# SBUF pools placed from both ends of the partition in a two-block float32 transformer kernel

## The chip, the core and the metric

The kernel runs on one NeuronCore of one Trainium2 chip. The metric is the time of one execution on the device in microseconds (us); less is better. Engines are named as in the profile: PE (TensorE matmuls), PEld (its weight loads), DVE (VectorE), ACT (ScalarE), POOL (GpSimd) and SP (the queue that issues most DMAs). SBUF addresses below are kilobytes (KB) from the start of a partition; every partition has the same layout.

## What is computed

One transformer block (differential attention and latent attention side by side, then a SwiGLU feed-forward) on 256 tokens of width 1024, and after it two layers of a second block. Everything is float32. Cut to its matrix products:

```python
z = rms_norm(x) @ w_in                      # q, k, v, latents, gates
y_a = merge_heads(diff_attention(z)) @ w_proj_a
y_b = merge_heads(latent_attention(z)) @ w_proj_b
x = x + rms_norm((sigmoid(g_a) * y_a + sigmoid(g_b) * y_b) @ w_o)
x = x + rms_norm((silu(n(x) @ w_ffn_gate) * (n(x) @ w_ffn_up)) @ w_ffn_down)
for i in range(2):                          # the second block's layers
    h = h + 0.5 * rms_norm(swiglu(n(h), gate[i, 0], up[i, 0], down[i, 0]))
    h = h + rms_norm((retention if i == 0 else stick_breaking)(n(h)))   # each ends in "@ w_out"
    h = h + 0.5 * rms_norm(swiglu(n(h), gate[i, 1], up[i, 1], down[i, 1]))
    h = h + rms_norm(sigmoid(n(h) @ ple_w_gate[i]) * (p[i] @ ple_w_proj[i]))
```

So there are five feed-forwards (hidden width 2816 = 22 x 128), and some 280 MB of weights go through the core once.

## The kernel before

**Three matmuls for one.** A float32 operand is split into two rounded halves of type float32r, `hi` and `lo`; a product is `hi*hi + hi*lo + lo*hi`, so three PE instructions in place of one. Weights come in chunks of 2048 columns (`chunk`): one DMA of 1 MB from SP into a buffer of the pool `raw` (3 buffers `w_raw`), then for each 512 columns a cast on ACT (L188) into `w_hi` (pool `hip`, 12 buffers) and a subtraction on DVE (L189) into `w_lo` (pool `lop`, 12 buffers).

**Two forms of product.** In the form by tokens (`tokens` and `token_steps`, instructions of L197) the stationary operand, the one that PE loads as weights, is 128x128 of the activations and the moving operand is 512 (sometimes 256) columns of `w_hi` or `w_lo`. In the form by features (`mat_steps`, L214) the weights are stationary and 256 tokens of the activations move. The names of the activations: `x_hi`/`x_lo` is the normed input of every stage, `a_*` the hidden layer of a feed-forward (stationary in the down-projection, 22 blocks x 2 token halves x 2 output halves x 3 = 264 instructions in each of five feed-forwards), `u_*` the retention's output, `o_*` the stick-breaking's, `oa_*` and `ob_*` the two attentions', `m_*` their sum, `pe_*` the extra embedding, `cq_*`/`ckv_*` the latents, `p_*` and `v_*` the retention's scores and values (there `v` moves). Full float32 matmuls are left for transposes (`xt`, `at`, `mt`, ...: the identity in `kc` moves, the tile to be turned is stationary) and for attention scores. `h` is the residual stream, read by the transposes of every stage.

**What sets the order.** The order on each engine is fixed when the program is built, by the place in the code and by priorities; tiles of a pool are handed out in that order, and a tile that takes the place of an older one waits until the older one's readers are done. Pools that stay for the whole program lie one behind the other from the low end in the order of their creation (`const`, `raw`, `hip`, `lop`, `act`, `sm`, `tmp`); the pools of a stage (`mix`, `big`, `ends`, `ret`, `stick`, `emb`) are stacked behind them, and dropped at the stage's end. `h` is a tile of `act`.

Of the kernel before, what the change touches and what calls it, by code (L numbers as in the profile page):

```python
# [10 lines left out]
F32 = mybir.dt.float32  # L11
# [7 lines left out]
P = 128  # L19
T = 256  # L20
D = 1024
# [73 lines left out]
class Weights:  # L95


    def __init__(self):
        self.parts = []
# [45 lines left out]
class Build:  # L145
    def __init__(self, ctx, tc, aps):
        self.ctx, self.tc, self.nc = ctx, tc, tc.nc
        self.aps = aps
        self.plan = []
        self.at = 0  # L150
        pool = lambda name, bufs, **k: ctx.enter_context(tc.tile_pool(name=name, bufs=bufs, **k))
        self.const = pool("const", 1)
        self.raw = pool("raw", 3)
        self.hip = pool("hip", WB)
        self.lop = pool("lop", WB)
        self.act = pool("act", 1)
        self.sm = pool("sm", 2)
        self.tmp = pool("tmp", 2)
        self.psm = pool("psm", 4, space=PSUM)
        self.psa = pool("psa", 4, space=PSUM)  # L160
        self.filler, self.behind, self.late = Filler(), None, []
        self.later = None
# [337 lines left out]

    def setup(self):
        nc, const, aps = self.nc, self.const, self.aps
        self.h = self.act.tile([P, 2, D], F32, name="h", tag="h")

        self.h0 = self.h.rearrange("p b d -> p (b d)").rearrange("p (k t) -> p k t", k=KT)
        self.vecs = const.tile([P, NV], F32, name="vecs")
        self.kc = const.tile([P, NK], F32, name="kc")
        nc.scalar.dma_start(self.kc[:, :P], aps["kc"][:, :P])
        nc.scalar.dma_start(self.vecs[:, :KT], aps["vecs"][:, :KT])
        self.pos = self.tmp.tile([P, T], I32, name="pos", tag="s")  # L510
        self.lam = self.tmp.tile([P, 4 * 64], F32, name="lam", tag="s")
        self.ident = self.kc[:, K_ID : K_ID + P]
        self.ones = const.tile([P, P], F32, name="ones")
        nc.vector.memset(self.ones, 1.0)
        self.dummies(WARM[0])
        self.mhalf = const.tile([P, 2], F32, name="mhalf")
        nc.vector.memset(self.mhalf, -0.5)
# [777 lines left out]
    def run(self):  # L1295
        tc = self.tc
        self.setup()
        g2 = lambda i, n: self.vec(V_G2 + (i * 8 + n) * 8, 8)
        row = lambda i, n: R_G2 + 4 * i + n // 2
        stage = self.first()  # L1300
        with tc.tile_pool(name="big0", bufs=1) as self.big:
            self.ffn(*stage, ("w_ffn_gate", "w_ffn_up", "w_ffn_down"), (0,), R_FFN, 1.0)
        names = ("ffn_w_gate_2", "ffn_w_up_2", "ffn_w_down_2")
        out = self.aps["out"].rearrange("p (b d) -> p b d", b=2)
        p_halves = self.ctx.enter_context(tc.tile_pool(name="p_halves", bufs=1))
        self.pe = [p_halves.tile([P, SUB], F32R, name=f"pe_{x}") for x in "hl"]
        pos = self.tmp.tile([P, T], I32, name="pos", tag="s")
        self.nc.gpsimd.dma_start(pos, self.aps["pos2"].to_broadcast([P, T]))
        self.table2 = self.rope_table("2", pos, self.kc[:, K_F2 : K_F2 + 1], self.const)
        for i in range(2):  # L1310
            with tc.tile_pool(name=f"big{i}a", bufs=1) as self.big:
                self.ffn(*self.next_stage(g2(i, 0)), names, (i, 0), row(i, 1), 4.0)
            self.later = lambda i=i: self.embed_in(i)
            mixer = self.stick if i else self.retention
            mixer(*self.next_stage(g2(i, 2)), row(i, 3))
            with tc.tile_pool(name=f"emb{i}", bufs=1) as emb:
                e = emb.tile([P, 2, D], F32, name="e")
                self.embed(i, e)
                with tc.tile_pool(name=f"big{i}b", bufs=1) as self.big:
                    self.ffn(*self.next_stage(g2(i, 4)), names, (i, 1), row(i, 5), 4.0)  # L1320
                self.ple(i, *self.next_stage(g2(i, 6), 4.0), e, row(i, 7), out if i else None)
        assert self.at == WCOLS * P, (self.at, WCOLS * P)
# [66 lines left out]
```

## Time and profile before

| | |
|---|---|
| median of 3 runs | 1613.9 us (1613.33 to 1614.34) |
| the profiled execution's own time | 1613.39 us |
| its span, first to last instruction | 1611.5 us |
| PE busy in the span | 1597.7 us (99%) |
| PE's share of the chain that ended last | 95% |
| DVE, ACT, POOL busy | 1065.2, 904.1, 79.9 us |
| DMA, mean | 179 GB/s |

The span is what the trace covers; about 2 us of the execution lie around it. Busy time of PE is the time in which a matmul was under way, and matmuls overlap (a 512-column one is shown with some 390 ns, though another starts every 230 ns), so a busy PE is not yet a PE at its best pace. Its pace is read from the starts of consecutive instructions in the timeline, or from a piece of the chain of work: a piece that is "x243" long and lasts 56.70 us takes 56.70 / 243 us for each instruction.

### The profile page before, as it was taken

To read this page: it belongs to the slowest core of one execution; us is meant where nothing else is said; L and a number is where in the kernel's file an instruction comes from. 1 tells how busy PE (TensorE), PEld (TensorE's weight loads), DVE (VectorE), ACT (ScalarE), POOL (GpSimd) and SP (SyncE) were. 2 spreads that over 40 slices of the span, in tenths; PEclk is the share of its full clock that TensorE was granted. 3 is DMA by queue.
4 is the path that set the end of the run, shared out by engine and by line. 5 is a ranking of instruction groups with operands and counts; after the bars stand their busy time and mean duration, and the time that the engine had idled before them with its cause. 6 is when DMAs were issued, how large, how long until landed. Compare 5 with 4: busy or idle time off the path is not lost.

```text
span 1611.5 us, 22515 instructions
## 1 busy us (share of the span) xinstructions
PE 1597.7 (99%) x8230; PEld 1344.3 (83%) x8230; DVE 1065.2 (66%) x1969; ACT 904.1 (56%) x1792; POOL 79.9 (5%) x97
## 2 busy tenths in 40 slices
PE   9999999999999999999999999999999999999997
PEld 8898778888888888898888888878888899888886
DVE  7987766765566665777766555486665677666546
ACT  6665544755455554645546555476554656655545
POOL 0000000200001000100000000012000200000001
PEclk9999999999999999999999999999999999999999
DMA  7535436455546555555455555555555554455552
GB/s 243 211 123 190 167 106 221 183 179 201 183 159 220 183 183 183 167 189 183 160 190 179 187 178 188 183 198 200 183 183 183 176 192 149 165 183 183 183 175 73
DMA packets 47134, 288.72 MB, mean 179 GB/s; under 512 B 5968, under 2 KB 9168, under 8 KB 14384
## 3 DMA queue, kind: packets, MB, share of 16 engines
q1 hardware_dynamic: 44528, 279.29, 49.3%
q0 software_dynamic: 2064, 7.80, 1.4%
q8 instruction: 64, 1.05, 0.3%
q14 instruction: 46, 0.38, 0.1%
q10 hardware_dynamic: 432, 0.20, 0.0%
HBM read 284.78 MB, written 1.05 MB: 177 GB/s over the span
## 4 chain that ended last, share of the span: by engine, by line
PE 95%; DVE 2%; DMA 1%; issue 1%; ACT 1%; SPq 0%; POOL 0%; POOLq 0%; DVEq 0%; ACTq 0%
PE ps L197 78%; PE ps L214 9%; PE at L628 1%; PE S L660 1%; PE xt L429 1%; DMA w_raw<-in_w 1%; DVE w_lo L189 1%; PE o L197 1%; PE o L707 0%; DMA h<-in_x 0%; PE S L1073 0%; PE S L1187 0%; PE pt L697 0%; PE o L834 0%; PE ot L1110 0%
## 5 line engine op out<-in xcount | busy, mean ns | idle before, releaser
L189 DVE TENSOR_TENSOR w_lo<-w_raw,w_hi 128x512 fp32r<-128x512 f32 x1054 | 708.8, 687 | 348.8 <-ACT w_hi L188 343.5
L188 ACT CAST w_hi<-w_raw 128x512 fp32r<-128x512 f32 x1054 | 639.6, 621 | 489.2 <-PE ps L197 355.8
L197 PE MATMUL ps<-w_hi,x_hi 128*128 128x512 f32 (+1 forms) x1280 | 488.9, 382 | 0.3 <-ACT x_hi L433 0.3
L197 PE MATMUL ps<-w_hi,x_lo 128*128 128x512 f32 (+1 forms) x1280 | 483.0, 377 | 0.5 <-DVE x_lo L435 0.5
L197 PE MATMUL ps<-w_lo,x_hi 128*128 128x512 f32 (+1 forms) x1280 | 482.1, 377 | 0.0
L197 PEld LDWEIGHTS ps<-w_hi,x_lo 128*128 128x128 f32 x1280 | 240.8, 188 | 46.9 <-DVE x_lo L435 2.1
L197 PEld LDWEIGHTS ps<-w_hi,x_hi 128*128 128x128 f32 x1280 | 241.0, 188 | 43.3 <-issue 1.0
L197 PEld LDWEIGHTS ps<-w_lo,x_hi 128*128 128x128 f32 x1280 | 241.2, 188 | 42.1
L197 PE MATMUL ps<-w_hi,a_hi 128*128 128x512 f32 x440 | 176.7, 402 | 0.0
L197 PE MATMUL ps<-w_hi,a_lo 128*128 128x512 f32 x440 | 173.3, 394 | 0.0
L197 PE MATMUL ps<-w_lo,a_hi 128*128 128x512 f32 x440 | 172.6, 392 | 0.0
L296 POOL TENSOR_TENSOR r<-v,mhalf 128x1 f32<-128x1 f32 (+1 forms) x50 | 61.4, 1228 | 1262.6 <-DVE v L384 1097.7
L214 PE MATMUL ps<-x_hi,w_hi 128*128 128x256 f32 x440 | 114.8, 289 | 0.7 <-ACT x_hi L356 0.5
L214 PE MATMUL ps<-x_hi,w_lo 128*128 128x256 f32 x440 | 112.5, 284 | 0.6 <-DVE w_lo L189 0.6
L197 PEld LDWEIGHTS ps<-w_hi,a_lo 128*128 128x128 f32 x440 | 82.6, 188 | 21.3
L197 PEld LDWEIGHTS ps<-w_lo,a_hi 128*128 128x128 f32 x440 | 82.7, 188 | 19.2
L197 PEld LDWEIGHTS ps<-w_hi,a_hi 128*128 128x128 f32 x440 | 82.6, 188 | 18.4
L214 PEld LDWEIGHTS ps<-x_hi,w_hi 128*128 128x128 f32 x440 | 84.0, 191 | 2.2 <-issue 0.7
L214 PEld LDWEIGHTS ps<-x_hi,w_lo 128*128 128x128 f32 x440 | 84.1, 191 | 1.5 <-DVE w_lo L189 1.2
L623 DVE SCALAR_TENSOR_TENSOR a<-ps,R,s 128x512 f32<-128x512 f32 (+1 forms) x60 | 42.2, 703 | 55.4 <-PE ps L197 44.0
L214 PE MATMUL ps<-x_lo,w_hi 128*128 128x256 f32 x440 | 77.4, 283 | 0.0
L270 ACT CAST a_hi<-at 128x512 fp32r<-128x512 f32 (+1 forms) x60 | 33.1, 551 | 70.4 <-PE at L628 70.4
(271 smaller groups left out, 1484.0 us busy)
## 6 DMA issues: line engine op xcount, KB each, us to landing
w_raw<-in_w SPq DMA_DIRECT2D x254, 1024.0 KB, 4.9
gr<-in_rows POOLq DMA_DIRECT2D x10, 512.0 KB, 4.1
w_raw<-in_w SPq DMA_DIRECT2D x7, 512.0 KB, 3.4
w_raw<-in_w SPq DMA_DIRECT2D x12, 256.0 KB, 5.1
w_raw<-in_w SPq DMA_DIRECT2D x6, 384.0 KB, 3.3
h<-in_x SPq DMA_DIRECT2D x4, 256.0 KB, 5.6
h<-in_x POOLq DMA_DIRECT2D x1, 1024.0 KB, 8.9
out<-h SPq DMA_DIRECT2D x3, 256.0 KB, 2.5
```

The costliest lines, as they stand in the source:

```text
L188: nc.scalar.copy(hi[:, :m], r[:, c0:c1])
L189: nc.vector.tensor_sub(lo[:, :m], r[:, c0:c1], hi[:, :m].bitcast(F32))
L197: mm = lambda a, b, **k: nc.tensor.matmul(ps, a, b, skip_group_check=True, **k)
L214: mm = lambda *a, **k: self.nc.tensor.matmul(*a, skip_group_check=True, **k)
L270: nc.scalar.copy(hi, src)
L296: self.nc.gpsimd.tensor_tensor(r, v, self.mhalf[:, :n], op=ALU.pow)
L429: nc.tensor.transpose(pt[:, i, :], self.h[:, b, k * P : (k + 1) * P], self.ident)
L623: nc.vector.scalar_tensor_tensor(a, banks[1], R[:, b : b + 1], s, op0=ALU.mult, op1=ALU.mult)
L628: nc.tensor.transpose(pt[:, i, :], a[:, i * P : (i + 1) * P], self.ident)
L660: mm(S[:, at], q[:, qs], k[:, ks], start=n == 0, stop=n == len(parts[0]) - 1, skip_group_check=True)
```

## The change

The pools are given a side. `hip`, `lop`, `act` and the pools of the stages stay on the left (the low end); `const`, `raw`, `sm`, `tmp`, `p_halves` (the tiles `pe_*`) and `emb` go to the right and are stacked from the high end down. `h` moves from `act` into a pool of its own, `res`, on the right. No instruction is added, removed or given another shape.

```diff
-        self.const = pool("const", 1)
-        self.raw = pool("raw", 3)
+
+        self.const = pool("const", 1, side="right")
+        self.raw = pool("raw", 3, side="right")
         self.hip = pool("hip", WB)
         self.lop = pool("lop", WB)
         self.act = pool("act", 1)
-        self.sm = pool("sm", 2)
-        self.tmp = pool("tmp", 2)
+        self.res = pool("res", 1, side="right")
+        self.sm = pool("sm", 2, side="right")
+        self.tmp = pool("tmp", 2, side="right")
...
-        self.h = self.act.tile([P, 2, D], F32, name="h", tag="h")
+        self.h = self.res.tile([P, 2, D], F32, name="h", tag="h")
...
-        p_halves = self.ctx.enter_context(tc.tile_pool(name="p_halves", bufs=1))
+        p_halves = self.ctx.enter_context(tc.tile_pool(name="p_halves", bufs=1, side="right"))
...
-            with tc.tile_pool(name=f"emb{i}", bufs=1) as emb:
+            with tc.tile_pool(name=f"emb{i}", bufs=1, side="right") as emb:
```

The addresses that the two built programs give to the tiles, in KB of a partition:

| tile | read by PE as | before | after |
|---|---|---|---|
| `kc` (identity), `ones` | moving, float32 | 16.8 to 17.9 | 220.8 to 221.9 |
| `w_raw` | (not by PE) | 20.0 to 44.0 | 196.1 to 220.1 |
| `w_hi` | moving (L197), stationary (L214) | 44.0 to 68.0 | 16.1 to 40.1 |
| `w_lo` | moving (L197), stationary (L214) | 68.0 to 92.0 | 40.1 to 64.1 |
| `h` | stationary, float32 | 92.0 to 100.0 | 188.1 to 196.1 |
| `x_hi`, `x_lo`; `ob_*` in the same place | stationary (L197), moving (L214) | 100.0 to 116.0 | 64.1 to 80.1 |
| `a_hi`, `a_lo` | stationary | from 133.1, 137.1 or 145.1, to 189.1 at most | 80.1 to 124.1 |
| `u_h`, `u_l` | stationary | 137.1 to 169.1 | 80.1 to 112.1 |
| `oa_h`, `oa_l` | stationary | 145.1 to 161.1 | 92.1 to 108.1 |
| `m_h`, `m_l` | stationary | 161.1 to 177.1 | 108.1 to 124.1 |
| `o_h`, `o_l` | stationary | 148.6 to 164.6 | 91.6 to 107.6 |
| `pe_h`, `pe_l` | stationary | 133.1 to 137.1 | 167.0 to 171.0 |
| `ckv_*` / `cq_*` | both / moving | 196.1 to 200.1 / 190.1 to 196.1 | 143.1 to 147.1 / 137.1 to 143.1 |
| retention's `p_*` / `v_*` | stationary / moving | 205.6 to 211.6 / 169.1 to 185.1 | 148.6 to 154.6 / 112.1 to 128.1 |
| `a` (before its transpose) | stationary, float32 | 181.1 to 197.1 | 128.1 to 132.1 |

On PE, DVE, ACT and SP the instructions stand in the same order in both programs. PE in the first feed-forward of the second block, with what it waits for in brackets (`at` is the transpose of the hidden layer; the numbers of lines are two higher in the changed file). Before:

```order
L197 MATMUL ps<-w_hi,x_hi 128x512
L197 MATMUL ps<-w_lo,x_hi 128x512
L197 MATMUL ps<-w_hi,x_lo 128x512
L628 MATMUL at<-kc,a 128x128 [waits DMASW3_49,DVE_49]
L628 MATMUL at<-kc,a 128x128 x3
L197 MATMUL ps<-w_hi,x_hi 128x512 [waits Activation_49]
```

After:

```order
L199 MATMUL ps<-w_hi,x_hi 128x512
L199 MATMUL ps<-w_lo,x_hi 128x512
L199 MATMUL ps<-w_hi,x_lo 128x512
L630 MATMUL at<-kc,a 128x128 [waits DVE_49]
L630 MATMUL at<-kc,a 128x128 x3
L199 MATMUL ps<-w_hi,x_hi 128x512 [waits Activation_49]
```

One wait for a DMA of POOL's queue (`DMASW`) is gone there; the tile `a` no longer lies where that DMA had written. POOL is the one engine with another order. It loads the gain rows of each stage (`gr`, 512 KB). Before, at the end of the first layer:

```order
L467 DMA gr<-in_rows 128x1024
L296 TENSOR_TENSOR r<-v_10532,mhalf 128x1
L467 DMA gr<-in_rows 128x1024 x2
L296 TENSOR_TENSOR r<-v_10630,mhalf 128x1
L453 COPY R<-r 128x1
```

After, the same place, and behind "..." the place at the end of the stick-breaking stage to which one of the two loads goes:

```order
L469 DMA gr<-in_rows 128x1024
L298 TENSOR_TENSOR r<-v_10535,mhalf 128x1
L469 DMA gr<-in_rows 128x1024
L298 TENSOR_TENSOR r<-v_10633,mhalf 128x1
...
L298 TENSOR_TENSOR r<-v_13824,mhalf 128x1
L469 DMA gr<-in_rows 128x1024
L298 TENSOR_TENSOR r<-v_13990,mhalf 128x1
```

It is the gain row of the last feed-forward, which is first read about 200 us behind the new place.

## Rows read from the trace of the kernel before

**Rows 1.** The page: busy time, granted clock in 40 slices, chain by engine.

```profile
PE 1597.7 (99%) x8230; PEld 1344.3 (83%) x8230; DVE 1065.2 (66%) x1969; ACT 904.1 (56%) x1792; POOL 79.9 (5%) x97
...
PEclk9999999999999999999999999999999999999999
...
PE 95%; DVE 2%; DMA 1%; issue 1%; ACT 1%; SPq 0%; POOL 0%; POOLq 0%; DVEq 0%; ACTq 0%
```

**Rows 2.** Waits of PE, the longest: total us, times, longest us.

```profile
PE dummy L522 <- DVE mhalf L517: 1.1, 1, 1.1
```

**Rows 3.** The chain of work, longest pieces: start us, us, what, how many.

```profile
418.01 56.70 PE ps L197 x243
...
821.08 48.06 PE ps L197 x206
```

**Rows 4.** The chain in 318 to 342 us, products with `x`.

```profile
317.85 16.32 PE ps L197 x72
```

**Rows 5.** The chain in 240 to 290 us: `ob`, then `m`.

```profile
243.61 1.40 PE ps L197 x6
245.66 8.88 PE ps L197 x39
...
268.11 17.50 PE ps L197 x75
```

**Rows 6.** Busy us (x instructions) PE, PEld, DVE, ACT, POOL; clock, DMA share, GB/s.

```profile
420.00:460.00 40.00, 40.00 (x173) 32.20 (x172) 20.14 (x30) 18.15 (x30) 0.00 (x0) 1.00 0.56 196
340.00:380.00 40.00, 40.00 (x184) 33.11 (x183) 22.85 (x34) 21.25 (x36) 0.00 (x0) 1.00 0.56 199
```

**Rows 7.** PE's groups by shape, xcount | busy us, mean ns | idle.

```profile
L197 PE MATMUL ps<-w_hi,x_hi 128*128 128x512 f32 x1120 | 442.9, 395 | 0.3 <-ACT x_hi L433 0.3
...
L197 PE MATMUL ps<-w_hi,a_hi 128*128 128x512 f32 x440 | 176.7, 402 | 0.0
...
L197 PE MATMUL ps<-w_hi,u_l 128*128 128x512 f32 x64 | 25.6, 400 | 0.0
```

**Rows 8.** Chain, short pieces: `oa`, `x`, `a` behind an interruption; then `o`, `pe`.

```profile
218.51 1.40 PE ps L197 x6
...
311.86 2.78 PE ps L197 x12
...
604.10 2.79 PE ps L197 x12
...
1371.96 17.06 PE ps L197 x73
```

**Rows 9.** Chain, other PE work: retention's `p`/`v`; transposes of `a`, of `h`; L214.

```profile
707.23 2.08 PE o L197 x9
...
311.42 0.44 PE at L628 x4
...
285.61 0.87 PE xt L429 x8
...
678.74 11.51 PE ps L214 x96
```

**Rows 10.** Timeline of PE, 166 to 168 us: `cq` moving, six instructions apart.

```profile
166.50 0.28 PE L214 MATMUL ps<-cq_h,w_hi 128*128 128x256 f32 x1
...
167.20 0.28 PE L214 MATMUL ps<-cq_h,w_hi 128*128 128x256 f32 x1
```

**Rows 11.** The page: cast, subtraction; weight DMAs (KB, us to landing).

```profile
L189 DVE TENSOR_TENSOR w_lo<-w_raw,w_hi 128x512 fp32r<-128x512 f32 x1054 | 708.8, 687 | 348.8 <-ACT w_hi L188 343.5
L188 ACT CAST w_hi<-w_raw 128x512 fp32r<-128x512 f32 x1054 | 639.6, 621 | 489.2 <-PE ps L197 355.8
...
w_raw<-in_w SPq DMA_DIRECT2D x254, 1024.0 KB, 4.9
```

**Rows 12.** Timeline of POOL at the end of the first layer.

```profile
1064.28 0.53 POOL L467 DMA_DIRECT2D gr<-in_rows  x1 [1.22 <-DVE h L415]
1064.82 0.82 POOL L296 TENSOR_TENSOR r<-v,mhalf 128x1 f32<-128x1 f32 x1
```

## The prediction

> **What bounds the kernel now.** The page comes first: PE is busy 1597.7 us of 1611.5, and the chain that ended last is PE for 95% [rows 1]. The longest wait of PE is 1.1 us [rows 2], so there is hardly a stall to remove. A change can gain only if PE's instructions themselves follow each other faster, or lose if they follow slower or begin to wait. So the next view is the pace of PE, and the chain gives it without any modelled end: length of a piece over its count. Four readings for the same shape, 128x128 stationary and 512 columns moving, all of line L197:
> - down-projection, `a` stationary: 56.70 / 243 = 233.3 ns [rows 3];
> - retention's output, `u` stationary: 48.06 / 206 = 233.3 ns [rows 3];
> - any product with `x` stationary: 16.32 / 72 = 226.7 ns [rows 4];
> - the two products of the first block's end, a few us apart and of the same form: `ob` 8.88 / 39 = 227.7 ns, `m` 17.50 / 75 = 233.3 ns [rows 5].
>
> At 2.4 GHz that is 544 cycles in the one kind and 560 in the other for 512 columns. The granted clock is 1.00 in a stretch of either kind, the DMA share 0.56 in both, and DVE and ACT are busier in the faster one (22.85 and 21.25 us of 40) than in the slower (20.14 and 18.15) [rows 6]; none of these makes the 6.7 ns. What does separate them is the address table: `x` and `ob` lie at 100 to 116 KB (and share their place), everything at 233.3 ns begins at 133 KB or above, while the moving `w_hi` and `w_lo` are the same tiles at 44 to 92 KB throughout. Shape does not separate them: `m`, `ob` and `x` are tiles of equal shape. I read this as 6.7 ns for each stationary operand that lies above some address between 116 and 133 KB while the moving one lies below it.
>
> **The change part by part.** *Stationary tiles that come down.* `a`, `u`, `m`, `o` and `oa` all end below 124.1 KB. Instructions: `a` 3 groups of 440 = 1320, `u` 3 of 64 = 192 (one group of each in [rows 7]); `oa`, `m` and `o` have 8 blocks, two token halves and two output halves, 3 x 32 = 96 each. The full price would be 1800 x 6.67 ns = 12.0 us. Not all of it comes: behind an interruption of the stream the first dozen run at one pace whatever the address. Twelve with `x` behind a transpose take 2.78 us, twelve with `a` 2.79 us; six with `oa` between attention work take 1.40 us [rows 8], and six with `ob`, at the low address, 1.40 us too [rows 5]. So by place: `a` loses one dozen in each of five feed-forwards, 1320 - 60 = 1260, worth 8.4 us; `u` runs in one piece, 192, 1.3 us; `m` about 85 of 96, 0.6 us; `o` about 55 of 96 (its last piece has 73 instructions with some of `pe` among them, 17.06 / 73 = 233.7 ns [rows 8]), 0.35 us; `oa` nothing. That is 10.6 us. Between 10.6 and the full 12.0 I take 11.0, near the low end because the rows with pieces of six and twelve speak for it. All of it lies on the path, since PE is the chain.
>
> *Tiles that stay above.* `pe` goes from 133 to 167 KB and `ckv` from 196 to 143: 48 and 24 instructions, no change. The retention's product with `p` stationary and `v` moving had both above 133 KB and took 2.08 / 9 = 231 ns [rows 9]; now `v` comes down and `p` stays. Bounds: nothing, or 36 x 2.3 ns = 0.1 us if it goes to 233.3. I take nothing.
>
> *Tiles that go up.* `h` becomes a stationary operand at 188 KB and the identity a moving one at 220 KB, in the 160 transposes of `h` and 220 of `a`. With the identity low, four transposes of `a` (181 KB) take 0.44 us, eight of `h` (92 KB) 0.87 us: 110 and 109 ns [rows 9]; the stationary address does not show in float32. For a moving operand that is high the nearest rows are `cq` at 190 KB: six instructions in 0.70 us, 117 ns [rows 10], against 11.51 / 96 = 120 ns with `x` at 100 KB [rows 9]. So no loss; the 1.3 ns between the two transposes, on 380 of them 0.5 us, is what I allow on either side.
>
> *Producers.* `w_raw` moves to 196 KB, where no weight DMA lands now. A faster PE asks for a chunk every 24 x 226.7 ns = 5.44 us in place of 5.60; a chunk costs DVE 4 x 687 = 2.7 us, ACT 4 x 621 = 2.5 us and 4.9 us from issue to landing with three buffers [rows 11]. The `x` stretches keep that very pace now, with PE never idle [rows 6], so the cover holds. It would be gone if a landing took about twice as long.
>
> *Queues.* PE, DVE, ACT and SP keep their order. On POOL one load of gain rows moves to the stick-breaking stage's end; behind it in the queue stands one `r` (for `R`, which is first wanted when the first hidden block is done). The same pair exists before: the load 0.53 us, then `r` at once, after a wait for DVE [rows 12], and no wait of PE answers to it. Nothing; 0.5 us if it were exposed. The waits that fall away on PE are for DMAs that landed long before.
>
> The sum against the profiled execution: 1613.39 - 11.0 = 1602.4 us. That execution is 0.5 us below the median of the runs, so against the median 1613.9 - 11.0 = 1602.9 us.
>
> **The rivals.** *Nothing happens.* The two paces could belong to the stages (their chunks, waits and neighbours) and not to the place. For it: place and stage were never varied apart for `a`, which holds most of the price. Against it: `ob` and `m`, neighbours of one form [rows 5], and `u` in a stage of its own with the very 233.3 ns of `a` [rows 3]. Time 1613.9. The Trainium skill leads to this rival: its page "SBUF — State Buffer", section "Who interferes with whom", says that TensorE has two independent read ports and never waits for another engine, and names no price for an address; its page "TensorE: Matmul & The Clock Gate", section "Back-to-back issue gap", gives N / 2.4 + 2.5 ns, 216 ns for 512 columns, wherever the operands lie. By these pages the change is worth 0. The rows differ from both, 226.7 and 233.3 ns for one shape [rows 3, 4].
>
> *Part of it.* The step lies between 116 and 124 KB and not at 128: then the upper blocks of `a_lo` and `m_l` keep the old price, at most 8 of 22 blocks, 160 + 32 instructions, 1.3 us. Time 1604.2.
>
> *Slower.* There is a second step, on the moving side below 44 KB, where no float32r operand lies now: 8 of the 12 places of `w_hi` are then below 32 KB. If what counts is how much farther the stationary operand is than the moving one, those matmuls would pay the 6.7 ns: 2/3 of the 512-column instructions move `w_hi`, 2/3 of these from such a place, so 4/9 of some 5330 (3 x 1120 with `x` [rows 7], 1970 others), 2370 x 6.67 = 15.8 us. Net 1613.9 + 15.8 - 11.0 = 1618.7. It decides the sign from 1650 such instructions on. Against it: `w_hi` lies on both sides of 64 KB now and `w_lo` up to 92, `x` from 100, and all of that runs at one pace, 226.7 ns [rows 4]; a step at each 32 KB would show there.
>
> **How the numbers follow.** Forecast 0.81, part of it 0.06, nothing 0.07, slower 0.06. A difference under about 0.2% (3.2 us) can hardly be told from no change here. Forecast and part are faster, 0.87; nothing is same, 0.07; slower 0.06. The range: below, the full 12.0 us, 0.5 us for transposes and 0.4 us for the spread of the runs, 1613.9 - 12.9 = 1601.0; above, the part case at 1604.2 with what I allowed for transposes, POOL and `p` (1.1 us) and about as much again for disturbances that the trace before cannot show, 1606.5. That leaves out the two cases of 0.07 and 0.06.
>
> **What would show it.** Right: the longest pieces of the chain, now 56.70 us for 243, take about 55.1 us (226.7 ns each) in all five feed-forwards, `u` 46.7 us for 206, `m` 17.0 for 75; `pe` stays at 233; pieces of `x` stay at 226.7. Wrong: the `a` pieces keep 56.7 us (nothing), or only the last blocks of `a` do (part), or `x` pieces rise with `w_hi` low (slower). PE waits that name `w_hi`, `w_lo` or `w_raw` would say that the producers' cover is gone.

## The result and the profile after

The changed kernel takes 1603.57 us (median; 1603.18 to 1603.95) beside 1613.73 us before on the same chip: ratio 0.9937, 95% interval 0.9919 to 0.9954. The profiled execution has a span of 1601.7 us, 9.8 less than before. The forecast was 1602.9.

Two rows of the page after: busy time, then the chain by engine.

```profile
PE 1586.9 (99%) x8230; PEld 1346.0 (84%) x8230; DVE 1063.9 (66%) x1969; ACT 904.8 (56%) x1792; POOL 79.8 (5%) x97
...
PE 95%; DMA 2%; DVE 1%; ACT 1%; issue 1%; SPq 0%; POOL 0%; POOLq 0%; DVEq 0%; ACTq 0%
```

As many PE instructions as in [rows 1], 10.8 us less busy time, and PE is still the chain. Where the time went is told by the chain after (start us, us, what, how many):

```profile
217.60 1.40 PE ps L199 x6
...
269.08 17.05 PE ps L199 x75
...
312.37 2.77 PE ps L199 x12
...
338.28 19.08 PE ps L199 x84
...
406.51 8.63 PE ps L199 x72
...
418.34 55.13 PE ps L199 x243
...
602.72 2.76 PE ps L199 x12
...
605.70 55.13 PE ps L199 x243
...
675.74 11.51 PE ps L216 x96
...
704.24 2.07 PE o L199 x9
...
817.78 46.87 PE ps L199 x206
...
1364.10 16.77 PE ps L199 x73
...
1512.19 55.13 PE ps L199 x243
```

The piece of `a`, 56.70 us before [rows 3], is 55.13 us, 226.9 ns each, in all five feed-forwards: 5 x 1.57 = 7.85 us. `u` went from 48.06 [rows 3] to 46.87, `m` from 17.50 [rows 5] to 17.05, the piece of `o` and `pe` from 17.06 [rows 8] to 16.77. Together 9.8 us. `x` keeps its pace (19.08 / 84 = 227.1 ns), and so do the short piece of `oa` (1.40 for six), the dozen with `x` behind a transpose (2.77), the retention's product (2.07 for nine) and the 256-column products: 8.63 / 72 = 119.9 ns for the tail of each feed-forward's `x` stretch, 11.51 / 96 for L216 (L214 before).

The start has become later: the piece of `a` begins at 418.34, 0.33 us behind the 418.01 of before, though `m` has gained 0.45 by then. The chain of the first 33 us after shows what PE waits for there:

```profile
20.64 8.15 DMA w_raw<-in_w
...
32.10 6.01 PE ps L216 x48
```

A landing of raw weights is on the chain. It does not go with the new places: in `all_but_raw` below, which has the raw weights at the low end again, the same landing takes 8.78 us and the 48 products begin at 32.78, and in `weights_high`, which has them exactly where they were before, 8.24 and 31.74 (31.41 in the kernel before). Executions of one kernel differ by as much: 25 of the kernel before lie between 1612.42 and 1615.08 us.

### The profile page after: what moved, and what is told of

Same layout as the page of the kernel before. It is cut to its first block, busy times and chain, and to the rows that moved or that the text cites. A ratio compares the mean times of both kernels' runs of the same rounds, so it can differ in the third digit from the quotient of the medians.

```text
span 1601.7 us, 22514 instructions
## 1 busy us (share of the span) xinstructions
PE 1586.9 (99%) x8230; PEld 1346.0 (84%) x8230; DVE 1063.9 (66%) x1969; ACT 904.8 (56%) x1792; POOL 79.8 (5%) x97
## 4 chain that ended last, share of the span: by engine, by line
PE 95%; DMA 2%; DVE 1%; ACT 1%; issue 1%; SPq 0%; POOL 0%; POOLq 0%; DVEq 0%; ACTq 0%
PE ps L199 78%; PE ps L216 9%; DMA w_raw<-in_w 2%; PE at L630 1%; PE S L662 1%; PE xt L431 1%; PE o L199 1%; PE o L709 0%; DVE w_lo L191 0%; ACT w_hi L190 0%; PE S L1075 0%; PE S L1189 0%; PE pt L699 0%; PE o L836 0%; PE ot L1112 0%
## 5 line engine op out<-in xcount | busy, mean ns | idle before, releaser
L199 PE MATMUL ps<-w_hi,a_hi 128*128 128x512 f32 x440 | 172.8, 393 | 0.0
L216 PE MATMUL ps<-x_hi,w_hi 128*128 128x256 f32 x440 | 114.7, 289 | 1.6 <-ACT x_hi L358 0.9
L216 PE MATMUL ps<-x_hi,w_lo 128*128 128x256 f32 x440 | 112.5, 284 | 0.2 <-DVE w_lo L191 0.2
L216 PEld LDWEIGHTS ps<-x_hi,w_hi 128*128 128x128 f32 x440 | 84.1, 191 | 2.9 <-ACT x_hi L358 1.1
L216 PEld LDWEIGHTS ps<-x_hi,w_lo 128*128 128x128 f32 x440 | 84.3, 192 | 0.8 <-DVE w_lo L191 0.5
L216 PE MATMUL ps<-x_lo,w_hi 128*128 128x256 f32 x440 | 77.5, 283 | 0.0
```

Source lines behind the costliest of these rows:

```text
L199: mm = lambda a, b, **k: nc.tensor.matmul(ps, a, b, skip_group_check=True, **k)
L216: mm = lambda *a, **k: self.nc.tensor.matmul(*a, skip_group_check=True, **k)
```

## The experiments

Three theories at first. **A** is the prediction's: 6.7 ns per matmul whose stationary tile lies above some address near 128 KB while the moving one lies below it. **B**: what counts is where the raw weights land. **C**: what counts is that the two operands lie on different sides, or far from each other.

**The raw weights alone to the right.**

```diff
-        self.raw = pool("raw", 3)
+        self.raw = pool("raw", 3, side="right")
```

> The kernel before with the pool raw alone on the right: w_hi 20 to 44 KB, w_lo 44 to 68, x 76 to 92, but a_hi from 109, 113 or 121 KB and a_lo from 131 to 143, so that a_hi crosses 128 KB within its 22 blocks of 1 KB and a_lo lies above. Theory A (a stationary operand above 128 KB, with a moving one below, costs 6.7 ns): within one down-projection the pace changes at the block that crosses 128 KB, about 226.7 ns below for the instructions with a_hi and dearer above; 1148 of before's 1872 such instructions stay, and at the 5.8 ns a piece that the change measured (10.2 us for 1764) the time is 1613.7 - 4.2 = 1609.5. Theory B (it is the way of the weights' raw buffers, written by DMA and read by ACT and DVE in the same half as PE's tiles, that slows PE): all of the gain, about 1603.5, and 226.7 ns in every block.

Measured 1613.61 us, ratio 1.0001 (0.9991 to 1.0010). Every lower tile comes down by 24 KB, so that a good part of `a_hi` now lies below 128 KB. Chain, the piece of `a` in the first feed-forward, then `u`:

```profile
419.05 56.70 PE ps L197 x243
...
822.11 48.07 PE ps L197 x206
```

No block of `a` became faster. A expected some 4 us, B all of the gain. Neither holds.

**All of the change but the raw weights** (which stay left, ahead of `hip`).

```diff
-        self.raw = pool("raw", 3, side="right")
+        self.raw = pool("raw", 3)
```

> The changed kernel with the pool raw back on the left: w_raw 16 to 40 KB, w_hi 40 to 64, w_lo 64 to 88, x 88 to 104, a_hi 104 to 126, a_lo 126 to 148. Theory A: instructions with a_hi at 226.7, those with a_lo from its third block on dearer, a down-projection at (2 x 226.7 + 233.3) / 3 = 228.9 ns a piece; 646 instructions stay above, so 1613.7 - 7.1 = 1606.6. Theory B: none of the gain, 1613.7, 233.3 ns throughout.

Measured 1601.98 us, ratio 0.9930 (0.9915 to 0.9945): all of the gain, although the operands lie 24 KB higher than in the changed kernel, and `a_lo` between 126 and 148 KB. Chain:

```profile
418.25 55.13 PE ps L199 x243
...
817.71 46.87 PE ps L199 x206
```

By A the upper tiles should have kept the old pace. B is out too.

**The rounded weights to the right in the kernel before** (the first two lines alone); **then the activations `x` as well** (all three).

```diff
-        self.hip = pool("hip", WB)
-        self.lop = pool("lop", WB)
-        self.act = pool("act", 1)
+        self.hip = pool("hip", WB, side="right")
+        self.lop = pool("lop", WB, side="right")
+        self.act = pool("act", 1, side="right")
```

> The kernel before with hip and lop alone on the right: w_lo 176 to 200 KB, w_hi 200 to 224; all else slides down, x 52 to 68, a_hi from 85, 89 or 97, a_lo from 107 to 119 KB. Now the moving operand of L197 is high and the stationary one low, and in L214 the stationary one is high and the moving one low. Theory A as the prediction has it (only a stationary operand farther than the moving one pays): L197 226.7 ns with x and a, 10.5 us less, and L214 from 120 to 126.7 ns, 1320 x 6.67 = 8.8 us more: 1612. Theory C (whenever the two lie on different sides of 128 KB): L197 at 233.3 with x too, 3360 + 480 instructions, some 24 us more, L214 8.8 us more: about 1648.

> hip, lop and act on the right: w_lo 176 to 200 KB, w_hi 200 to 224, x 160 to 176, h 152 to 160; a, u, oa, m, o all below 117 KB. So x and the weights are both high, in both forms of product, and a is low under high weights. Theory A by difference (only a stationary operand above while the moving one is below): 226.7 ns with x and with a, L214 120 ns, all of the gain: about 1604. Theory A by place (a stationary operand above 128 KB pays wherever the moving one is): x at 233.3 ns, 3360 + 480 + 96 instructions or some 25 us, L214 126.7 ns, 8.8 us, less 10.5 us for the rest: about 1637. Theory C (different sides): x at 226.7, a at 233.3 as before, about 1614.

Measured 1613.97 (1.0002, 0.9993 to 1.0012) and 1614.01 us (1.0004, 0.9995 to 1.0013). In the second, `a`, `u`, `oa`, `m` and `o` end by 117.1 KB, with the weights at the high end. A piece of `x` and the piece of `a` in the one, then the piece of `a` in the other:

```profile
338.32 19.10 PE ps L197 x84
...
418.51 56.70 PE ps L197 x243
```

```profile
417.88 56.70 PE ps L197 x243
```

Not one phase has another pace than before. The times alone would not tell: the first is near A's 1612, a sum of a gain and a loss of which neither came, and the second is what C expected. The paces do: in the first, `a` should have become fast by A, and `x` slow by C. Which region or side a tile is in, and how far the operands are apart, does not show at all. A, B and C have all fallen.

**A new theory from the addresses, this time to the byte.** The table ahead of the prediction gives KB to one decimal. The bytes above a whole KB are these:

```
                          w_hi, w_lo   x, ob   a, u, m, oa, cq   o     pe
before, and the three
 kernels at its pace         992         992        128          640   128
after, and all_but_raw       128         128        128          640   992
```

Before, the small constants end 32 bytes short of a KB and shift `raw`, `hip`, `lop` and `act` with them, while the odd sizes in `sm` bring the stage pools back to 128. In the changed kernel constants and `sm` are on the other side, and everything that PE multiplies starts at 128 but `pe`. Theory **D**: a float32r matmul of 512 columns follows the one ahead at 226.7 ns when its two operands start at the same offset modulo a small power of two, and at 233.3 when not. Its rival **E**: it is the new grouping of the pools by sides after all. Below, d is the start of the activation tile less that of the weight tile, modulo 256 bytes.

**One temporary of the kernel before made longer**, nothing moved between sides:

```diff
-        rh = self.sm.tile([P, 2], F32, name="rh", tag="rh", bufs=1)
+        rh = self.sm.tile([P, 96], F32, name="rh", tag="rh", bufs=1)[:, :2]
```

> The kernel before with one small tile of the pool sm made 352 bytes longer; every pool and tile stays on its side and in its order, and only the stage pools move up by 352 bytes. Theory D (the low bits: a float32r matmul of 512 columns takes 560 cycles when its stationary tile and its moving tile start at different offsets within a small power of two of bytes, 64 to 512, and 544 when at the same one; before, w and x start at 992 bytes above a whole KB and the stage pools at 128, a difference of 864; here 1216, so the difference is 512 bytes less than a whole KB): all of the gain, chain pieces of a near 55.1 instead of 56.70, u near 46.9 instead of 48.06, pe at 226.7 instead of 233 ns, the 256-column matmuls over cq at 120 instead of 117.4; 1872 matmuls by 6.67 ns is 12.5, less 0.4 for cq and ckv, and some of it lies under waits as it did in the changed kernel: 1602.5 (1601.5 to 1604). Rival E (it is the pools' sides after all: constants and temporaries out from between the operands): nothing changes its side, 1613.6 and 56.70.

Measured 1603.11 us, ratio 0.9937 (0.9919 to 0.9955): the whole effect of the change, from 352 bytes of padding. Chain, `x`, `a` and `u`:

```profile
337.40 19.10 PE ps L197 x84
...
417.57 55.10 PE ps L197 x243
...
817.08 46.75 PE ps L197 x206
```

The stage tiles lie above 133 KB, as before; they now start 480 bytes above a whole KB and the weights 992, which is a difference of 512 (the 1216 in the expectation is a slip). E is out.

**Thirty-two bytes into the changed kernel**, between the weights and everything they meet:

```diff
+        pad = pool("pad", 1).tile([P, 8], F32, name="pad")
+        self.nc.gpsimd.memset(pad, 0.0)
         self.act = pool("act", 1)
```

> The changed kernel with a pad of 32 bytes between the pools lop and act, so that x and every stage tile start 32 bytes further from w than they did; sides and order are those of the changed kernel (one memset of 32 bytes a partition is added on POOL at the start). Theory D: every 512-column matmul with w moving turns slow, x (3360) too, which was fast in all kernels so far: 5280 by 6.67 ns is 35.2 more; the 256-column matmuls with w stationary, 1476, turn from 120 to 117.4 as cq's did before, which gives back 3.8: 1603.6 + 31.4 = 1635 (1632 to 1639), pace of x 233.3. If the 256-column ones stay at 120, 1638.8. Rival E (sides): 1603.6, pace of x 226.7, chain pieces of a 55.13.

Measured 1627.34 us, ratio 1.0085 (1.0067 to 1.0103): slower than the kernel before. Chain of the first feed-forward (`x` with 512 columns, with 256, then `a`) and of the retention's L218 (weights stationary):

```profile
316.46 19.59 PE ps L201 x84
...
409.52 8.52 PE ps L201 x72
...
421.28 56.69 PE ps L201 x243
...
684.50 11.20 PE ps L218 x96
```

`x`, fast in every kernel so far, takes 19.59 / 84 = 233.2 ns, `a` 233.3. With 256 columns it goes the other way, as `cq` did before: 8.52 / 72 = 118.3 ns in place of 119.9, and L218 11.20 / 96 = 116.7 in place of 119.9. The direction was right and the size was not, 24 us in place of 31. I had charged every 512-column matmul. In the first 240 us, where attention work interrupts the stream and the products wait, nothing was lost on balance, and `oa` never had the fast pace to lose; from 289 us on, five `x` stretches lose 2.6 us each and five of `a` 1.6, which is 21, and the retention's `x`, `u` and `o`, less what the 256-column products give back, add the other 3.

**Pads of 64 bytes ahead of `act` and of 64 behind it.**

```diff
+        pad = pool("pad", 1).tile([P, 16], F32, name="pad")
+        self.nc.gpsimd.memset(pad, 0.0)
         self.act = pool("act", 1)
+        pad = pool("pad2", 1).tile([P, 16], F32, name="pad2")
+        self.nc.gpsimd.memset(pad, 0.0)
```

> The changed kernel with a pad of 64 bytes ahead of the pool act and another of 64 behind it: x starts 64 bytes and the stage tiles 128 bytes further from w (two memsets on POOL at the start). It tells the period of theory D. Period 64 bytes: nothing changes, 1603.6, x and a at 226.7. Period 128: x slow (3360 by 6.67 ns = 22.4, less some 3.4 from 256-column matmuls over x at 117.4), a fast: 1622.6. Period 256 or 512: x and a both slow, 1635. Rival E: 1603.6, as with a period of 64.

Measured 1625.38 us in one run. The same four pieces, `x` now at d = 64 and `a` at d = 128:

```profile
317.07 19.60 PE ps L203 x84
...
410.09 8.18 PE ps L203 x72
...
421.51 56.48 PE ps L203 x243
...
683.93 11.30 PE ps L220 x96
```

Both slow: 233.3 and 232.4 ns. So the period is neither 64 nor 128. The paces decide this and not the time, which lies nearer to the 1622.6 of a period of 128 than to 1635: as with 32 bytes, not every matmul pays the full price. With 256 columns, d = 64 gives 8.18 / 72 = 113.6 ns, the fastest seen.

**A different offset in every phase.** Each weight tile gets 512 bytes of room, and `chunk` writes the weights a number of bytes into it that depends on the matrix.

```diff
-WB = 12
+WB = 10
...
-            hi = self.hip.tile([P, SUB], F32R, name="w_hi", tag="a")
-            lo = self.lop.tile([P, SUB], F32R, name="w_lo", tag="b")
+            o = self.offset(blocks[0]) // 4
+            hi = self.hip.tile([P, SUB + ROOM], F32R, name="w_hi", tag="a")[:, o : o + SUB]
+            lo = self.lop.tile([P, SUB + ROOM], F32R, name="w_lo", tag="b")[:, o : o + SUB]
```

> The changed kernel with room of 512 bytes in every w_hi and w_lo tile (ten buffers of each in place of twelve) and the weights of each phase written a number of bytes into the tile, so that w stands that many bytes above the activation it meets. 512-column matmuls over x in the five feed-forwards: 16, 256, 128, 448, 480; over a: 256, 384, 8, 64, 192; over ob, m, u, o: 0. 256-column ones over x: 64, 128, 256, 384, 16 in the five feed-forwards. Weights stationary: 32 in the first phase, 64, 128, 256, 384 in the four heads of the retention, 16 then 192 in the stick-breaking. Theory D with a period of 512 bytes: every 512-column phase whose offset isn't 0 at 232 to 234 ns, chain pieces of a 56.5 to 56.7, m and u as in the changed kernel; 3720 such by 6.5 ns is 24 more, some 5 less from 256-column ones: about 1622.5. With a period of 256: the first feed-forward's a and the second's x, at 256, at 226.7, 5 less: about 1618. If it is the 32 bytes alone that count, 8 and 16 would be fast. Which offset is best for 256-column matmuls is open: 113.6 (x 64 above w) is the best so far, 120 at 0.

Measured 1617.10 us in one run. Chain; the offsets of the weights in these rows are, from the top, 16 (`x`), 64 (`x`, 256 columns), 256 (`a`), 256 (`x`), 128 (`x`, 256 columns), 384 (`a`), 64, 256 and 384 (L242, weights stationary), 128 (`x`), 8 (`a`), 64 (`a`), 16 (`x`, 256 columns), 192 (`a`). As the weights stand above the activation here, d is 256 minus the offset, or 512 minus the offset where that is 256 or more:

```profile
315.69 19.46 PE ps L225 x84
...
408.21 8.48 PE ps L225 x72
...
419.90 55.14 PE ps L225 x243
...
504.50 19.07 PE ps L225 x84
...
595.44 8.54 PE ps L225 x72
607.20 56.48 PE ps L225 x243
...
678.57 11.31 PE ps L242 x96
...
742.47 11.51 PE ps L242 x96
...
780.32 11.53 PE ps L242 x96
...
896.32 19.60 PE ps L225 x84
...
1001.35 56.70 PE ps L225 x243
...
1219.07 55.64 PE ps L225 x243
...
1512.47 8.54 PE ps L225 x72
...
1524.25 56.71 PE ps L225 x243
```

256 is as good as 0 (226.9 ns with `a`, 227.0 with `x`), and eight bytes are enough to lose it (56.70). The period is 256 bytes, the second of the cases that were written down ahead of the run, and the time is within 1 us of the 1618 given for it. Not every other offset costs the 232 to 234 ns expected: 16 bytes (d = 240) gave 231.7 and 64 (d = 192) only 229.0. Pace in ns by d, from this kernel and the ones ahead:

| form | d = 0 | 32 | 64 | 128 | 160 | 192 | 240 | 248 |
|---|---|---|---|---|---|---|---|---|
| 512 columns, activation stationary | 226.9 | 233.2 | 233.3 | 232.4 with `a`, 233.3 with `x` | 233.3 | 229.0 | 231.7 | 233.3 |
| 256 columns, activation stationary | 119.9 | 118.3 | 113.6 | 118.6 | | 117.8 | 118.6 | |
| 256 columns, weights stationary | 119.9 | 116.7 | 117.7 | 120.1 | 117.4 | 117.8 | | |

**Each form at its best offset**, from the changed kernel with raw weights and `p_halves` on the left, and from `before_shifted_352`:

```diff
-WB = 12
+WB = 11
...
+            o = {P: 56, 256: 48}.get(len(blocks[0][3]), 0)
-            hi = self.hip.tile([P, SUB], F32R, name="w_hi", tag="a")
-            lo = self.lop.tile([P, SUB], F32R, name="w_lo", tag="b")
+            hi = self.hip.tile([P, SUB + 64], F32R, name="w_hi", tag="a")[:, o : o + SUB]
+            lo = self.lop.tile([P, SUB + 64], F32R, name="w_lo", tag="b")[:, o : o + SUB]
```

> The changed kernel with the raw weights back on the left (as all_but_raw, 1601.98), the pool of pe on the left too (so that it stands at w's offset), 256 bytes of room in every weight tile (eleven buffers in place of twelve) and the weights of a chunk written at the offset that the runs so far found best for its form: 0 for 512 columns, 192 bytes (w above x) for the 256 columns of the feed-forwards, 224 where the weights are stationary. Theory D: 480 matmuls of 256 columns at 113.6 in place of 119.7 give 2.9, 1476 with stationary weights at 116.8 in place of 119.9 give 4.6, some of it under the waits of the first 170 us, pe 48 by 7 ns gives 0.3, and the 512-column ones stay at 226.7: 1601.98 - 7 = 1595 (1594 to 1597.5). Rival E (sides): 1602, nothing changes its pace.

> The kernel before with every pool on its side, the stage pools 352 bytes up (as before_shifted_352, 1603.1) and the same room and offsets in the weight tiles, x and the stage tiles having the same offset as w again. Theory D: 2.9 + 4.6 less some under waits, 1603.1 - 7 = 1596 (1595 to 1598.5), the same paces as in three_offsets_left, though not one pool has changed its side. Rival E (sides): 1613.6.

Measured 1596.58 us, ratio 0.9896 (0.9880 to 0.9913), and 1598.18 us, ratio 0.9905 (0.9890 to 0.9919): both inside the ranges given, both faster than either of the two kernels of this case, and the second has no pool on another side than before. Chain of the first, then of the second:

```profile
311.96 19.07 PE ps L200 x84
...
402.86 8.18 PE ps L200 x72
...
414.23 55.12 PE ps L200 x243
...
671.05 11.20 PE ps L217 x96
```

```profile
404.49 8.48 PE ps L198 x72
...
416.19 55.13 PE ps L198 x243
...
673.48 11.20 PE ps L215 x96
```

A weight tile has 2304 bytes here, so that every other buffer is 256 bytes off modulo 512; `a` keeps its 55.12 and 55.13 over all of them, a second sign that the period is 256.

One number doesn't repeat: the 256-column products with `x` have d = 64 in both, and take 113.6 ns here and 8.48 / 72 = 117.8 there. On 480 instructions that is 2.0 us, about the difference of the two kernels. For this form something besides d counts. With 113.6 ns `w` starts at 64 bytes modulo 256 (here) or at 128 (the kernel with two pads), with 117.8 at 160; no run varies that alone, and what it is stays open.

## Why the number was right and the reason wrong

**What bounds the kernel.** Right: PE is the chain and hardly waits, so only its pace can change, and the pace of a long piece of the chain shows a change of 3% where busy time, whose ends are modelled, shows it less plainly.

**The step that failed** is the sentence "What does separate them is the address table". Everything at 233.3 ns lay above 133 KB, and everything at 226.7 below 116, but the two groups differed in a second thing, the bytes above a whole KB, and a table in tenths of a KB hides it (43.96875 stands there as 44.0). In the kernel before, the pools that were slow were those behind `sm`, high *and* shifted. The change ended both at once, so the result could not tell them apart; `before_shifted_352` (tiles above 133 KB, offset equal, fast) and `weights_and_x_high` (tiles low, offset unequal, slow) did. It was a cause argued from a split into two groups, for which the trace of before had no row with the one property and not the other.

**The sum.** The count was right, since the price per instruction was measured and the tiles that would change were the same under either reason. In the long pieces came, for `a`, 7.85 of 8.4; `u` 1.2 of 1.3; `m` 0.45 of 0.6; `o` 0.3 of 0.35; `oa` 0 of 0. The short pieces have the rest. The dozen with `a` behind a transpose took 2.79 [rows 8] and takes 2.76, so that "one pace whatever the address" was near and not exact; the 24 behind the long piece, nine of them with `a`, took 5.53 and take 5.45 in the first feed-forward. The piece of `m` begins at 269.08 in place of 268.11 [rows 5], 0.97 us later, and the span ends 9.8 earlier: from there on 10.8 us were gained, some tenths of them in `x`, between the 10.6 and the 11.0 of the sum, and the later start, which is within the spread of executions, took 1 us back.

**Luck.** That the sum came out is luck in one respect. The prediction does not look at the starts; that the weights came to begin 128 bytes above a whole KB, like the stage pools, is a by-product of moving the constants away from below them. With 32 bytes more between `lop` and `act` the same reasoning would have given the same 1602.9, and 1627.3 was measured.

**Tiles that stay above.** `pe` kept 234 ns as said, but since it has the one odd offset now (992 against 128), not for its height; in `before_shifted_352` and in both last kernels, where it is aligned, it has 227. The 46.7 us forecast for the 206 of `u` overlooked that some 20 of these are with `pe`: 46.87 in the changed kernel, 46.75 in `before_shifted_352`. The retention's product was 2.08 [rows 9] and is 2.07.

**Tiles that go up.** The transposes were rightly put at nothing. `cq` was not read as far as it goes: 117 ns beside the 120 of `x` [rows 9, 10] was the same effect with the other sign, and I took it only as a sign that height does no harm. In the changed kernel six instructions take 0.72 us, as this timeline of PE shows (start us, us, engine, line):

```profile
165.83 0.28 PE L216 MATMUL ps<-cq_h,w_hi 128*128 128x256 f32 x1
...
166.55 0.28 PE L216 MATMUL ps<-cq_h,w_hi 128*128 128x256 f32 x1
```

This is a loss of 156 x 2.5 ns = 0.4 us at most, and the one row of before that pointed to the offset from a second side.

**Producers and queues.** Right: the landing of a full chunk is 4.8 us after, 4.9 before [rows 11], the waits of PE after add up to 1.2 us at one place at most, and none of them names the moved load of POOL.

**The rivals.** "Nothing" had the strongest argument against my reason, that place and stage were never varied apart, and I gave it 0.07 on the strength of `ob` and `m`, which differ in offset as well. The Trainium skill led to it, by its pages "SBUF — State Buffer" (section "Who interferes with whom") and "TensorE: Matmul & The Clock Gate" (section "Back-to-back issue gap"). The first names no price for an address in TensorE's reads; the rows of `after_shifted_32` show one of 6 ns for 32 bytes. The second gives 216 ns for 512 columns, as the gap of an isolated matmul, and about 131 in a sustained stream; the fastest long piece of any run here has 226.7. "Part of it" is refuted by a piece of `a` that runs at one pace from end to end, "slower" by `x`, which kept 227 ns with `w_hi` low. A slower case did exist, 1627 us, and it needed 32 bytes in one place, between `lop` and `act`; nothing in my list of rivals stood for it.

## What to carry to other kernels

Before a difference in pace is put down to where a tile lies, write its start and that of its partner to the byte, and modulo 32 to 512 bytes as well. In a kernel that is bound by TensorE with float32r operands, give both operands the same start modulo 256 bytes for 512-column matmuls, and try a shift of 32 or 64 bytes between them for 256-column ones. A tile of a few bytes that stands between the two operands in a pool stack moves one against the other, so that an edit of a temporary can change the time: 352 bytes gave 0.6% here, 32 bytes cost 1.5%.

## What the runs showed of the hardware that was not expected

Two float32r matmuls of the same shape, at granted clock 1.0, follow at 226.7 ns (544 cycles at 2.4 GHz) when the starts of stationary and moving operand agree modulo 256 bytes, and mostly at 233.3 (560 cycles), from 231.7 to 234, at the other offsets tried but one: d = 192 takes 229.0. A difference of 8 bytes is enough. With 256 columns the order is reversed: 119.9 ns when they agree, 116.7 to 118.6 at most other offsets (120.1 at d = 128 with stationary weights), 113.6 at d = 64 with a stationary activation in two kernels and 117.8 at the same d in a third. Neither the distance of the operands nor their region or side made any difference in the kernels that varied them. What in the chip makes the difference, no run here shows.
